# Seven block products for w_down in groups 2, 4 and 6 of a two-layer hybrid model in fp32

## The chip, the cores and the metric

The kernel runs on one core of a Trainium2 chip. The metric is the device time of one execution in microseconds (us); of several runs the median is given. The core has a matrix engine (PE, with its weight loads shown apart as PEld), a vector engine (DVE), a scalar engine (ACT), GpSimd (POOL) and a sync engine (SP). Each of them takes its own instructions in order. Transfers from memory are issued by SP or, where they add to what already lies in the target, by POOL.

## What is computed

The reference has two layers over x of 512 tokens by 1024 channels, all in fp32. In each layer a projection `w_in` feeds three mixers (mLSTM, differential attention, HGRN2), whose outputs go through `w_out` and are added to x. Then comes the part that the change touches:

```python
h2 = rmsnorm(x, norm2_g[l])
a = jnp.square(jax.nn.relu(jnp.einsum('btd,df->btf', h2, w_up[l])))
x = x + jnp.einsum('btf,fd->btd', a, w_down[l])
```

`w_up` is 1024 x 4096 and `w_down` 4096 x 1024. Every matrix product is made of three passes: each operand is split into a rounded part (hi, type fp32r) and the remainder (lo), and hi*hi, hi*lo and lo*hi are summed in PSUM.

## The kernel before

**Jobs and panels.** The work on weights is a list of jobs in a fixed order (the loop at the end of the kernel function). Each job multiplies by one panel of weights, 128 x 1024 fp32 (512 KB). The loop prepares panel n + 2 and then runs job n. Preparing means: SP loads the panel into a raw buffer, ACT rounds it to `whi` in two halves (line 243), DVE subtracts to get `wlo` in two halves (line 244). There are three buffers of `whi` and `wlo`, so that the ACT cast for job n + 2 can start when PE has ended job n - 1. A raw buffer is free again once DVE has made `wlo` from it. Preparation and the DVE additions out of PSUM have high priority in the order of instructions that the program writes for each engine.

**The feed-forward part.** The 4096 inner channels are cut into 8 groups of 512. Group 0 of `w_up` is an ordinary product (`up_first`). Groups 1 to 7 (`up_group`) use a seven-product block scheme in place of eight: 512 tokens are two halves, 512 channels two halves, 1024 inputs two halves; seven products of 256 x 512 x 256 with sums and differences of blocks. The sums of the activation blocks are made once per layer (`blocks`, names b11, t1, t2, ...). The sums of the weight blocks are made in the raw buffer by transfers that POOL issues with an add (`block_panel`, line 262): buffer `mA` holds w11 and then w11 + w21, buffer `kT` holds w21 + w22, then + w11, then + w12. Each of the two tags is a pair of halves, and group g uses half g % 2 of both, so that two groups in a row use different halves. The order of the seven products is p1, p5, p2, p7, p6, p4, p3. A product is 24 matmuls of 256 columns (lines 1130 to 1132) into PSUM tags `hx`, `ax` or `pv`; DVE adds it to others in `tmp`; and `relu2` (lines 1087 to 1091) does relu and square on ACT, a cast to `ah` on ACT and the remainder `al` on DVE. `S["ah"]` and `S["al"]` have two places, for even and odd groups.

**w_down.** `down_group` is an ordinary product by `nat_pair`: 4 panels, each a job of 24 matmuls of 512 columns (`nat_mm`, lines 295 to 297). Two jobs in a row sum in the same four PSUM tiles (tag `mm`, 4 buffers), which DVE adds to x at the end of the second (`add_rows`, line 1002).

**Order.** Jobs of down group g (letter d) and up group g + 1 (letter u) are interleaved by a string from `ORDER`: the first for g = 0, the second for g = 1 to 5, the third for g = 6; the four down jobs of group 7 stand alone.

Functions that have to be run between jobs (the block sums of `blocks`) stand in a list `steps`, of which one is run after each job.

Of the kernel before, what the change touches and what calls it, by code (L numbers as in the profile page):

```python
# [8 lines left out]
F32 = mybir.dt.float32  # L9
F32R = mybir.dt.float32r  # L10
U8 = mybir.dt.uint8
AF = mybir.ActivationFunctionType
# [3 lines left out]
P = 128  # L16
# [12 lines left out]
S4 = 1024  # L29
WP = 1056  # L30
WARM = 2
TOP = 1 << 24
ORDER = ("duduuduuduu", "uuduudududu", "uuuduuduudd")
RB = 3
COLS = dict(mq=0, mk=256, mv=512, mo=768, aq=1032, ak=1544, av=2056, hq=2568, hf=2824, hi=3080)

# [26 lines left out]
def hybrid_kernel(ctx, tc, x, norm1_g, w_in, conv_w, gate_b, mlstm_g, qn_g, kn_g, lam_v, subln_g,  # L63
                  lb_param, hgrn_g, w_out, norm2_g, w_up, w_down, cst, msk, out):
    nc = tc.nc
# [17 lines left out]
    xs = [pool.tile([P, D], F32, name=f"x{i}", tag=f"x{i}") for i in range(NT)]  # L83
# [19 lines left out]
    def pair(tag, dt=F32):  # L103

        return sb([P, 2 * S4], tag, dt)
# [137 lines left out]
            nc.scalar.copy(hi[:, ch], raw[:, ch])  # L243
            V.tensor_sub(lo[:, ch], raw[:, ch], hi[:, ch].bitcast(F32))  # L244

    def block_panel(raw, fresh, add):


        hi = sb([P, WP], "whi", F32R, bufs=3)
        lo = sb([P, WP], "wlo", F32R, bufs=3)  # L250

        def v3(t):
            return t[:, 0:S4].rearrange("p (k n) -> p k n", n=256)
# [495 lines left out]
    jobs = []  # L749
# [3 lines left out]
    steps = []  # L753

    def add_layer(l):
        S = {}
# [327 lines left out]

        NG = DFF // 512

        def relu2(src, r, q, ah, al):
            act(r, src, AF.Relu)
            act(q, r, AF.Square)
            nc.scalar.copy(ah, q)  # L1090
            V.tensor_sub(al, q, ah.bitcast(F32))

        def up_first():
            def ev(base):
                def f(pt, c, tok):
                    if base + c == 0 and tok.start == 0:
                        S["ah"] = [sb([P, 4, T], y, F32R) for y in HT[0:2]]
                        S["al"] = [sb([P, 4, T], y, F32R) for y in HT[2:4]]
                    relu2(pt, slab(0, T, off=T * c)[:, tok], slab(1, T, off=T * c)[:, tok],
                          S["ah"][0][:, base + c, tok], S["al"][0][:, base + c, tok])  # L1100
                return f
            for a in range(2):
                t_group(w_up, KT, a * 256, lambda: S["h2"], ev(2 * a), 2)

        def up_group(g):
# [8 lines left out]
            def raw(tag):  # L1114
                if "raw_" + tag not in S:
                    S["raw_" + tag] = pair(tag)
                return S["raw_" + tag][:, g % 2 * S4:(g % 2 + 1) * S4]

            def in_ring():
                return sb([P, WP], "wraw", bufs=2)  # L1120

            def product(wt, name, tag):
                pt = ps(tag)
                wh, wl = wt
                hh, hl = S["F"][name]
                for c in range(2):
                    col = slice(c * P, (c + 1) * P)
                    dst = pt[:, c * 256:(c + 1) * 256]
                    for k in range(4):
                        mm(dst, wh[:, k, col], hh[:, k], start=k == 0, stop=False)  # L1130
                        mm(dst, wh[:, k, col], hl[:, k], start=False, stop=False)  # L1131
                        mm(dst, wl[:, k, col], hh[:, k], start=False, stop=k == 3)  # L1132
                return pt

            def put(src, i, j):

                n = 2 * i + j
                tok = slice(j * 256, (j + 1) * 256)

                def two(v):  # L1140
                    return v.rearrange("p (c t) -> p c t", c=2)
                relu2(two(src), two(slab(0, 512, off=512 * (n % 2))), two(slab(1, 512, off=512 * (n % 2))),
                      S["ah"][g % 2][:, 2 * i:2 * i + 2, tok], S["al"][g % 2][:, 2 * i:2 * i + 2, tok])

# [12 lines left out]

            def p6(wt):
                V.tensor_sub(tmp[1], product(wt, "t2", "hx"), tmp[0])
                V.tensor_add(tmp[2], st["7"], tmp[1])  # L1160
                V.tensor_sub(tmp[0], tmp[2], st["5"])
                V.tensor_sub(tmp[3], st["5"], tmp[1])
                put(tmp[0], 1, 1)

            def p4(wt):
                if g == 4 and l + 1 < DEPTH:
                    load_gains(l + 1)
                    prms[l + 1] = load_params(l + 1)()
# [7 lines left out]
            return [((lambda: block_panel(raw("mA"), w[1, 1], [])), p1),  # L1176
                    ((lambda: block_panel(raw("kT"), w[2, 1], [w[2, 2]])), p5),
                    ((lambda: block_panel(in_ring(), w[1, 2], [])), p2),
                    ((lambda: block_panel(raw("mA"), None, [w[2, 1]])), p7),
                    ((lambda: block_panel(raw("kT"), None, [w[1, 1]])), p6),  # L1180
                    ((lambda: block_panel(in_ring(), w[2, 2], [])), p4),
                    ((lambda: block_panel(raw("kT"), None, [w[1, 2]])), p3)]
# [15 lines left out]
        up_first()  # L1198
        for g in range(NG):
            n = len(jobs)  # L1200
            down_group(g)
            if g + 1 < NG:
                down = jobs[n:]
                del jobs[n:]
                up = [(prep, None, None, go) for prep, go in up_group(g + 1)]
                for s in ORDER[min(g, 1) if g + 2 < NG else 2]:
                    jobs.append((up if s == "u" else down).pop(0))

    for l in range(DEPTH):
        add_layer(l)  # L1210
# [51 lines left out]
```

## Time and profile before

| | |
|---|---|
| median of 3 runs | 1284.72 us (1284.5 to 1285.47) |
| the profiled execution | 1284.39 us |
| its span, first to last instruction | 1282.6 us |
| granted TensorE clock | 1.00 of full speed |
| PE busy | 1271.0 us, 7492 matmuls |
| DVE busy | 914.8 us, 2064 instructions |
| ACT busy | 713.2 us, 1537 instructions |
| moved | 140.83 MB, of that 29.36 MB by POOL's queue |

The profiled execution is 1.8 us longer than its span and 0.33 us below the median. Busy time is the time in which an engine has at least one instruction under way. Matmuls overlap, so that the distance from one start to the next, not the length of one, tells what a matmul costs.

### The profile page before, as it was taken

The numbers are of one execution on the slowest core, as the hardware profiler recorded it, in microseconds if no ns is written. First come the engines' busy times: TensorE is split into PE (matmuls) and PEld (weight loads), VectorE is DVE, ScalarE is ACT, GpSimd is POOL, SyncE is SP. The second block draws the span as 40 slices with busy tenths as digits, with TensorE's granted clock in tenths as the row PEclk, the third lists the DMA queues.
The fourth block names the chain that finished last, engine by engine and source line by source line (L and its number), as shares of the span: only waits on it lengthen the run. The fifth ranks groups of instructions, "written<-read, shape, count | busy, mean of one in ns | idle before, by whom it ended". The sixth has DMA issues, their size and how long they took to land.

```text
span 1282.6 us, 20019 instructions
## 1 busy us (share of the span) xinstructions
PE 1271.0 (99%) x7492; PEld 1090.1 (85%) x7492; DVE 914.8 (71%) x2064; ACT 713.2 (56%) x1537; POOL 91.4 (7%) x92
## 2 busy tenths in 40 slices
PE   8999999999999999999999999999999999999998
PEld 6788777888999899889877887788898988898886
DVE  6786887978866666766567767878897657565763
ACT  6754875638655445445456557756485544444551
POOL 0000000000111111100000000000010111011100
PEclk9999999999999999999999999999999999999999
DMA  6222211226577576735323221112356765575552
GB/s 209 83 66 80 58 43 43 76 70 165 121 167 147 140 165 148 151 100 119 108 83 85 64 83 50 50 39 78 98 133 134 164 163 131 149 164 132 111 134 85
DMA packets 110228, 140.83 MB, mean 110 GB/s; under 512 B 5354, under 2 KB 79668, under 8 KB 110132
## 3 DMA queue, kind: packets, MB, share of 16 engines
q1 hardware_dynamic: 80228, 109.66, 28.0%
q0 software_dynamic: 29568, 29.36, 15.6%
q8 instruction: 59, 0.97, 0.3%
q10 hardware_dynamic: 336, 0.54, 0.1%
q14 instruction: 37, 0.30, 0.1%
HBM read 137.45 MB, written 2.10 MB: 109 GB/s over the span
## 4 chain that ended last, share of the span: by engine, by line
PE 88%; DVE 5%; ACT 4%; DMA 1%; issue 1%; SPq 0%; POOL 0%; ACTq 0%; DVEq 0%; POOLq 0%
PE pmm L295 15%; PE pmm L297 15%; PE pmm L296 15%; PE pmm L303 3%; PE pmm L304 3%; PE pax L1131 3%; PE pmm L302 3%; PE pax L1132 3%; PE pax L1130 3%; PE pax L685 2%; PE phx L1132 2%; PE ppv L1131 2%; PE phx L1131 2%; PE phx L1130 2%; PE ppv L1130 2%; PE ppv L1132 2%
## 5 line engine op out<-in xcount | busy, mean ns | idle before, releaser
L243 ACT CAST whi<-wraw 128x512 fp32r<-128x512 f32 x216 | 123.3, 617 | 181.6 <-PE pmm L297 140.5
L244 DVE TENSOR_TENSOR wlo<-wraw,whi 128x512 fp32r<-128x512 f32 x216 | 140.5, 688 | 75.7 <-ACT whi L243 75.7
L295 PE MATMUL pmm<-whi,h 128*128 128x512 f32 (+2 forms) x496 | 192.0, 387 | 0.2 <-ACT h L341 0.2
L296 PE MATMUL pmm<-wlo,h 128*128 128x512 f32 (+2 forms) x496 | 189.8, 383 | 0.0
L297 PE MATMUL pmm<-whi,h 128*128 128x512 f32 (+2 forms) x464 | 177.8, 383 | 0.0
L286 ACT ACTIVATE whi<-wraw,gcol 128x256 fp32r<-128x256 f32 (+2 forms) x192 | 99.5, 572 | 82.5 <-PE pmm L297 64.6
L287 DVE SCALAR_TENSOR_TENSOR wlo<-wraw,gcol,whi 128x256 fp32r<-128x256 f32 (+2 forms) x192 | 101.9, 570 | 47.8 <-ACT whi L286 46.1
L1002 DVE TENSOR_TENSOR x<-x,pmm 128x512 f32<-128x512 f32 x144 | 98.7, 686 | 45.5 <-PE pmm L297 43.4
L295 PEld LDWEIGHTS pmm<-whi,h 128*128 128x128 f32 x496 | 93.3, 188 | 16.9 <-ACT h L341 0.6
L296 PEld LDWEIGHTS pmm<-wlo,h 128*128 128x128 f32 x496 | 93.3, 188 | 16.7 <-issue 0.2
L297 PEld LDWEIGHTS pmm<-whi,h 128*128 128x128 f32 x464 | 87.2, 188 | 16.3
L295 PE MATMUL pmm<-whi,yb 128*128 128x512 f32 (+2 forms) x256 | 100.4, 392 | 0.0
L296 PE MATMUL pmm<-wlo,yb 128*128 128x512 f32 (+2 forms) x256 | 98.6, 385 | 0.0
L296 PE MATMUL pmm<-wlo,ya 128*128 128x512 f32 (+2 forms) x240 | 92.1, 384 | 0.0
L295 PE MATMUL pmm<-whi,ya 128*128 128x512 f32 (+2 forms) x240 | 92.1, 384 | 0.0
L297 PE MATMUL pmm<-whi,yd 128*128 128x512 f32 (+2 forms) x224 | 86.2, 385 | 0.0
L297 PE MATMUL pmm<-whi,yc 128*128 128x512 f32 (+2 forms) x224 | 85.6, 382 | 0.0
L262 POOL DMA_DIRECT2D kT<-in_w_up_dram x42 | 55.6, 1325 | 400.2 <-DVE wlo L244 241.7
L243 ACT CAST whi<-kT 128x512 fp32r<-128x512 f32 x84 | 48.0, 619 | 61.5 <-PE pmm L297 30.6
L1130 PE MATMUL phx<-mid,whi 128*128 128x256 f32 x224 | 63.0, 281 | 0.0
L1131 PE MATMUL phx<-mid,whi 128*128 128x256 f32 x224 | 62.9, 281 | 0.0
L1132 PE MATMUL phx<-mid,wlo 128*128 128x256 f32 x224 | 62.9, 281 | 0.0
(465 smaller groups left out, 3309.1 us busy)
## 6 DMA issues: line engine op xcount, KB each, us to landing
wraw<-in_w_down_dram SPq DMA_DIRECT2D x64, 512.0 KB
wraw<-in_w_in_dram SPq DMA_DIRECT2D x51, 512.0 KB
kT<-in_w_up_dram POOLq DMA_DIRECT2D x42, 512.0 KB, 6.2
wraw<-in_w_up_dram SPq DMA_DIRECT2D x36, 512.0 KB
wraw<-in_w_out_dram SPq DMA_DIRECT2D x16, 512.0 KB
mA<-in_w_up_dram SPq DMA_DIRECT2D x14, 512.0 KB
kT<-in_w_up_dram SPq DMA_DIRECT2D x14, 512.0 KB
mA<-in_w_up_dram POOLq DMA_DIRECT2D x14, 512.0 KB, 6.1
```

The lines of the kernel that those rows point to most:

```text
L243: nc.scalar.copy(hi[:, ch], raw[:, ch])
L244: V.tensor_sub(lo[:, ch], raw[:, ch], hi[:, ch].bitcast(F32))
L262: nc.gpsimd.dma_start(out=v3(raw), in_=rows(b), accum_op=ALU.add)
L286: act(hi[:, ch], raw[:, ch], AF.Copy, scale=g)
L287: V.scalar_tensor_tensor(lo[:, ch], raw[:, ch], g, hi[:, ch].bitcast(F32), op0=ALU.mult, op1=ALU.subtract)
L295: mm(pt[:, :n], sh(a), wh[:, b], start=first and j == 0, stop=False)
L296: mm(pt[:, :n], sh(a), wl[:, b], start=False, stop=False)
L297: mm(pt[:, :n], sl(a), wh[:, b], start=False, stop=last and j == nk - 1)
L1002: V.tensor_add(xs[i][:, cols], xs[i][:, cols], pt)
L1130: mm(dst, wh[:, k, col], hh[:, k], start=k == 0, stop=False)
L1131: mm(dst, wh[:, k, col], hl[:, k], start=False, stop=False)
L1132: mm(dst, wl[:, k, col], hh[:, k], start=False, stop=k == 3)
```

## The change

Down groups 2, 4 and 6 (`SEVEN`) are made by seven block products too (`down_seven`). The activations of the group are four blocks A11, A12, A21, A22 of 256 channels x 256 tokens, the panel of weights four blocks of 256 x 512. Each product is a job (letter s) of 12 matmuls of 512 columns, two PSUM tiles of tag `mm`. Three of the seven go straight to x, four go to accumulators `acc(0)` to `acc(3)` in SBUF, which sum over the three groups: in group 2 ACT copies them there, in groups 4 and 6 DVE adds. After group 6 two steps (`s0`, `s1`) combine the accumulators and add them to x.

`up_group` of an even group leaves the squared activations in `a4` in fp32; only two blocks are split at once, the block differences and sums are made by DVE and split (ACT cast and DVE remainder) at the end of p3 and of the first four down products. `S["ah"][0]` is cut into four places for them. In odd groups the square is made in place.

Raw buffers: the pair of halves is now `raw(0)`, `raw(1)` (first halves of `mA` and `kT`) for the up groups, which swap roles from group to group, and `raw(2)`, `raw(3)` (second halves) for the down groups. The order of the up products is p5, p1, p2, p7, p6, p4, p3. `ORDER` has a string for each g.

```diff
-ORDER = ("duduuduuduu", "uuduudududu", "uuuduuduudd")
+SEVEN = (2, 4, 6)
+ORDER = ("duduuduuduu", "uuduudududu", "usuusuusuus", "ususududusudud", "usuusuusuus", "ususududusudud", "usuusuusuus",
+         "sssdddd")
...
+        def split(ah, al, q):
+            nc.scalar.copy(ah, q)
+            V.tensor_sub(al, q, ah.bitcast(F32))
...
+        def raw(n):
+            t = ("mA", "kT")[n % 2]
+            if "raw_" + t not in S:
+                S["raw_" + t] = pair(t)
+            return S["raw_" + t][:, n // 2 * S4:(n // 2 + 1) * S4]
...
-                relu2(two(src), two(slab(0, 512, off=512 * (n % 2))), two(slab(1, 512, off=512 * (n % 2))),
-                      S["ah"][g % 2][:, 2 * i:2 * i + 2, tok], S["al"][g % 2][:, 2 * i:2 * i + 2, tok])
+                r = slab(0, 512, off=512 * (n % 2))
+                act(r, src, AF.Relu)
+                if g in SEVEN:
+                    act(a4()[:, n], r, AF.Square)
+                    if n in (0, 2):
+                        split(*place(n // 2), a4()[:, n])
+                else:
+                    act(r, r, AF.Square)
+                    split(S["ah"][1][:, 2 * i:2 * i + 2, tok], S["al"][1][:, 2 * i:2 * i + 2, tok], two(r))
...
                 put(tmp[3], 0, 1)
+                if g in SEVEN:
+                    a = a4()
+                    V.tensor_sub(a[:, 0], a[:, 0], a[:, 1])
+                    split(*place(2), a[:, 0])
+                    V.tensor_sub(a[:, 1], a[:, 1], a[:, 3])
+                    split(*place(3), a[:, 1])
...
+            one, two_ = (0, 1) if g % 2 else (1, 0)
+            return [((lambda: block_panel(raw(two_), w[2, 1], [w[2, 2]])), p5),
+                    ((lambda: block_panel(raw(one), w[1, 1], [])), p1),
                     ((lambda: block_panel(in_ring(), w[1, 2], [])), p2),
+                    ((lambda: block_panel(raw(one), None, [w[2, 1]])), p7),
+                    ((lambda: block_panel(raw(two_), None, [w[1, 1]])), p6),
                     ((lambda: block_panel(in_ring(), w[2, 2], [])), p4),
+                    ((lambda: block_panel(raw(two_), None, [w[1, 2]])), p3)]
+        def down_seven(g):
...
+            def product(wt, n, to, after=None):
+                hi, lo = (t.rearrange("p (k t) -> p k t", k=2) for t in place(n))
+                for c in range(2):
+                    pt = ps("mm")
+                    tok = slice(c * P, (c + 1) * P)
+                    nat_mm(pt, 512, lambda k: hi[:, k, tok], lambda k: lo[:, k, tok], *wt,
+                           [(0, 0), (1, 1)], True, True)
+                    with tc.high_priority():
+                        if isinstance(to, tuple):
+                            i, j = to
+                            d = xs[2 * j + c][:, i * 512:(i + 1) * 512]
+                            V.tensor_add(d, d, pt)
+                        elif g == SEVEN[0]:
+                            nc.scalar.copy(acc(to)[:, c], pt)
+                        else:
+                            V.tensor_add(acc(to)[:, c], acc(to)[:, c], pt)
+                if after:
+                    after()
...
+            return [(pan(one, w[1, 1], []), None, None, lambda t: product(t, 0, 0)),
+                    (pan(in_ring, w[1, 2], []), None, None, lambda t: product(t, 1, (0, 0), t2)),
+                    (pan(two, w[2, 1], [w[2, 2]]), None, None, lambda t: product(t, 2, 1, t4)),
+                    (pan(one, None, [w[2, 1]]), None, None, lambda t: product(t, 3, 3, b22)),
+                    (pan(two, None, [w[1, 1]]), None, None, lambda t: product(t, 0, 2)),
+                    (pan(in_ring, w[2, 2], []), None, None, lambda t: product(t, 1, (1, 0))),
+                    (pan(two, None, [w[1, 2]]), None, None, lambda t: product(t, 2, (0, 1), add_up))]
```

Here `t2` and `t4` are one DVE sum and one split each, `b22` one split; `one` is `raw(2)` and `two` is `raw(3)`. After group 6 `add_up` puts into `steps` two functions: `s0` with six DVE additions of 512 columns and one subtraction of 1024, `s1` with six of 512 and one of 1024.

## Rows read from the trace of the kernel before

**Rows 1.** The page: busy time of each engine and chain that ended last.
```profile
PE 1271.0 (99%) x7492; PEld 1090.1 (85%) x7492; DVE 914.8 (71%) x2064; ACT 713.2 (56%) x1537; POOL 91.4 (7%) x92
...
PE 88%; DVE 5%; ACT 4%; DMA 1%; issue 1%; SPq 0%; POOL 0%; ACTq 0%; DVEq 0%; POOLq 0%
```

**Rows 2.** Stretches of two groups each: busy us (instructions), clock, DMA share, GB/s.
```profile
core 0: us, PE busy (x) PEld busy (x) DVE busy (x) ACT busy (x) POOL busy (x), PEclk, DMA share, GB/s
...
494.00:578.00 84.00, 84.00 (x530) 75.73 (x529) 52.48 (x83) 40.13 (x71) 9.00 (x7) 1.00 0.62 138
...
1134.00:1218.00 84.00, 84.00 (x530) 75.34 (x529) 52.56 (x83) 40.22 (x71) 9.01 (x7) 1.00 0.58 133
```

**Rows 3.** Timeline of PE: first up job, then a down job, in layer 0 (start, length).
```profile
332.38 0.28 PE L1130 MATMUL phx<-mid,whi 128*128 128x256 f32 x1
...
335.22 0.40 PE L295 MATMUL pmm<-whi,h 128*128 128x512 f32 x1
...
340.76 0.28 PE L1130 MATMUL pax<-mid,whi 128*128 128x256 f32 x1
```

**Rows 4.** Timeline of ACT, then DVE, then POOL's queue: one panel's preparation.
```profile
408.27 1.14 ACT L243 CAST whi<-kT 128x512 fp32r<-128x512 f32 x2 [2.70 <-PE pmm L297]
...
408.93 1.29 DVE L244 TENSOR_TENSOR wlo<-kT,whi 128x512 fp32r<-128x512 f32 x2
...
410.52 1.28 POOL L262 DMA_DIRECT2D kT<-in_w_up_dram  x1 [3.02 <-DVE wlo L244]
```

**Rows 5.** Timeline of DVE: instructions that start one after the other without a wait.
```profile
480.21 0.69 DVE L1160 TENSOR_TENSOR big<-pax,big 128x512 f32<-128x512 f32 x1
480.93 0.69 DVE L1161 TENSOR_TENSOR big<-big,pax 128x512 f32<-128x512 f32 x1
481.54 0.69 DVE L1162 TENSOR_TENSOR big<-pax,big 128x512 f32<-128x512 f32 x1
```

**Rows 6.** Groups of DVE, 409 to 493 us: busy, mean ns, idle before and releaser.
```profile
L244 DVE TENSOR_TENSOR wlo<-wraw,whi 128x512 fp32r<-128x512 f32 x24 | 15.5, 686 | 8.7 <-ACT whi L243 8.7
L1002 DVE TENSOR_TENSOR x<-x,pmm 128x512 f32<-128x512 f32 x15 | 10.3, 686 | 4.3 <-PE pmm L297 4.2
...
L1091 DVE TENSOR_TENSOR h<-big,h 128x512 fp32r<-128x512 f32 x8 | 5.5, 691 | 6.9 <-ACT h L1090 6.9
L1152 DVE TENSOR_TENSOR big<-ppv,big 128x512 f32<-128x512 f32 x2 | 1.4, 692 | 1.8 <-PE ppv L1132 1.8
```

**Rows 7.** Timeline of ACT: cast of a panel, then relu, square, cast.
```profile
444.63 1.14 ACT L243 CAST whi<-mA 128x512 fp32r<-128x512 f32 x2 [1.57 <-PE ppv L1131]
445.68 0.63 ACT L1088 ACTIVATE big<-big 128x512 f32<-128x512 f32 x1
446.34 0.63 ACT L1089 ACTIVATE big<-big 128x512 f32<-128x512 f32 x1
```

**Rows 8.** Timeline of POOL, then of DVE, at the start of the feed-forward part, layer 0.
```profile
306.35 1.43 POOL L262 DMA_DIRECT2D kT<-in_w_up_dram  x1 [59.34 <-DVE wlo L287]
...
324.67 1.29 DVE L1043 TENSOR_TENSOR mid<-big,mid 128x512 fp32r<-128x512 f32 x2
325.87 1.22 DVE L1059 TENSOR_TENSOR big<-big 128x1024 f32<-128x1024 f32 x1
```

**Rows 9.** Timeline of POOL, and stretches around it (columns as in rows 2).
```profile
446.94 1.28 POOL L262 DMA_DIRECT2D mA<-in_w_up_dram  x1 [18.31 <-DVE wlo L244]
448.15 1.38 POOL L262 DMA_DIRECT2D kT<-in_w_up_dram  x1
...
449.00:455.00 6.00, 6.00 (x48) 5.79 (x47) 4.42 (x7) 3.10 (x6) 1.83 (x2) 1.00 1.16 171
...
459.00:461.00 2.00, 2.00 (x11) 1.60 (x10) 1.29 (x2) 0.83 (x2) 0.00 (x0) 1.00 0.87 298
```

**Rows 10.** Line 262 as a whole: from issue to landing.
```profile
DMA to landing us min/median/max: 6.0/6.2/12.7
```

**Rows 11.** Timeline of ACT: the cast that follows the transfer into `mA` of rows 9.
```profile
458.69 1.14 ACT L243 CAST whi<-mA 128x512 fp32r<-128x512 f32 x2 [1.15 <-PE pax L1131]
```

More of the change, by code (lines that the diff above doesn't have):

```diff
@@ L244, in halves, with block_panel @@
             V.tensor_sub(lo[:, ch], raw[:, ch], hi[:, ch].bitcast(F32))
-    def block_panel(raw, fresh, add):
+    def block_panel(raw, fresh, add, n=256):
         hi = sb([P, WP], "whi", F32R, bufs=3)
@@ L252, in v3 @@
         def v3(t):
-            return t[:, 0:S4].rearrange("p (k n) -> p k n", n=256)
+            return t[:, 0:S4].rearrange("p (k n) -> p k n", n=n)
         def rows(b):
@@ L1089, in relu2 @@
             act(q, r, AF.Square)
-            nc.scalar.copy(ah, q)
-            V.tensor_sub(al, q, ah.bitcast(F32))
+            split(ah, al, q)
         def up_first():
@@ L1103, in up_first, with in_ring, a4, place @@
                 t_group(w_up, KT, a * 256, lambda: S["h2"], ev(2 * a), 2)
+        def in_ring():
+            return sb([P, WP], "wraw", bufs=2)
+        def a4():
+            return slab(2, 2 * S4, (4, 512))
+        def place(n):
+            return S["ah"][0][:, n], S["al"][0][:, n]
+        def acc(n):
+            return slab((1, 4, 5, 6)[n], S4, (2, 512))
+        def raw(n):
[3 more added lines that the diff above has]
+            return S["raw_" + t][:, n // 2 * S4:(n // 2 + 1) * S4]
         def up_group(g):
@@ L1112, in up_group @@
             tmp = [slab(13 + n // 2, 512, off=512 * (n % 2)) for n in range(4)]
[L1114 to L1120, printed above, removed]
             def product(wt, name, tag):
@@ L1174, in p3 @@
                 put(tmp[3], 0, 1)
-            return [((lambda: block_panel(raw("mA"), w[1, 1], [])), p1),
-                    ((lambda: block_panel(raw("kT"), w[2, 1], [w[2, 2]])), p5),
+                if g in SEVEN:
[5 more added lines that the diff above has]
+            one, two_ = (0, 1) if g % 2 else (1, 0)
@@ L1178, in up_group @@
+            return [((lambda: block_panel(raw(two_), w[2, 1], [w[2, 2]])), p5),
+                    ((lambda: block_panel(raw(one), w[1, 1], [])), p1),
                     ((lambda: block_panel(in_ring(), w[1, 2], [])), p2),
-                    ((lambda: block_panel(raw("mA"), None, [w[2, 1]])), p7),
-                    ((lambda: block_panel(raw("kT"), None, [w[1, 1]])), p6),
+                    ((lambda: block_panel(raw(one), None, [w[2, 1]])), p7),
+                    ((lambda: block_panel(raw(two_), None, [w[1, 1]])), p6),
@@ L1181, in up_group, with t2, t4, b22 @@
                     ((lambda: block_panel(in_ring(), w[2, 2], [])), p4),
-                    ((lambda: block_panel(raw("kT"), None, [w[1, 2]])), p3)]
+                    ((lambda: block_panel(raw(two_), None, [w[1, 2]])), p3)]
+        def down_seven(g):
+            w = {(i, j): w_down[l, g * 512 + (j - 1) * 256:g * 512 + j * 256, (i - 1) * 512:i * 512]
+                 for i in (1, 2) for j in (1, 2)}
+            def product(wt, n, to, after=None):
[16 more added lines that the diff above has]
+                    after()
+            def t2():
+                a = a4()
+                V.tensor_add(a[:, 0], a[:, 0], a[:, 3])
+                split(*place(0), a[:, 0])
+            def t4():
+                a = a4()
+                V.tensor_sub(a[:, 0], a[:, 2], a[:, 0])
+                split(*place(1), a[:, 0])
+            def b22():
+                split(*place(2), a4()[:, 3])
+            def add_up():
+                def to_x(i, j, op, n):
+                    for c in range(2):
+                        d = xs[2 * j + c][:, i * 512:(i + 1) * 512]
+                        op(d, d, acc(n)[:, c])
+                def s0():
+                    to_x(0, 0, V.tensor_add, 0)
+                    V.tensor_sub(acc(2), acc(2), acc(0))
+                    to_x(0, 1, V.tensor_add, 1)
+                    to_x(0, 1, V.tensor_sub, 2)
+                def s1():
+                    V.tensor_add(acc(3), acc(3), acc(2))
+                    to_x(1, 0, V.tensor_add, 3)
+                    to_x(1, 1, V.tensor_add, 3)
+                    to_x(1, 1, V.tensor_sub, 1)
+                if g == SEVEN[-1]:
+                    steps.extend([s0, s1])
+            def pan(r, fresh, add):
+                return lambda: block_panel(r(), fresh, add, 512)
+            one, two = (lambda: raw(2)), (lambda: raw(3))
+            return [(pan(one, w[1, 1], []), None, None, lambda t: product(t, 0, 0)),
[5 more added lines that the diff above has]
+                    (pan(two, None, [w[1, 2]]), None, None, lambda t: product(t, 2, (0, 1), add_up))]
@@ L1198, in add_layer @@
         up_first()
+        todo = dict(u=[], d=[], s=[])
         for g in range(NG):
-            n = len(jobs)
-            down_group(g)
-            if g + 1 < NG:
[L1203 to L1207, printed above, removed]
+            if g in SEVEN:
+                todo["s"] += down_seven(g)
+            else:
+                n = len(jobs)
+                down_group(g)
+                todo["d"] += jobs[n:]
+                del jobs[n:]
+            if g + 1 < NG:
+                todo["u"] += [(prep, None, None, go) for prep, go in up_group(g + 1)]
+            jobs.extend(todo[s].pop(0) for s in ORDER[g])
     for l in range(DEPTH):
```

## The prediction

> **What bounds the kernel now.** First the page: PE is busy for 99% of the span and the chain that ended last lies on PE for 88% [rows 1]. Busy is no proof that PE is the limit, since matmuls overlap; so next the stretches of the feed-forward part. Over two groups (84 us) PE is busy all the time at full clock, while DVE works 52.5 us (83 instructions) and ACT 40 us [rows 2]. Then the timeline of PE: an up job starts at 332.38, the down job behind it at 335.22, the next at 340.76 [rows 3]. So an up job (24 matmuls of 256 columns) takes 2.84 us and a down job (24 of 512) 5.54 us, or 0.231 us a matmul. Seven up and four down jobs make 7 x 2.84 + 4 x 5.54 = 42.04 us, which is half of the 84 us of two groups: PE has no gap there. A matmul taken away from this part is worth 0.231 us, as long as nothing else comes to be late.
>
> How much room the others have is read from one panel's preparation: the cast starts when PE frees a buffer at 408.27, DVE ends at 410.22, POOL issues the next addition at 410.52 [rows 4]. That is 1.95 us, inside the two jobs (5.6 us) that run between the freeing and the panel's own job. 3.7 us are spare.
>
> **PE.** A down group had 4 x 24 = 96 matmuls of 512 columns; seven products have 7 x 12 = 84. 12 fewer, in 3 groups and 2 layers: 72 x 0.231 = 16.6 us saved. An s job takes 12 x 0.231 = 2.77 us.
>
> **DVE and ACT.** Per group of the new kind: seven panels in place of four give 6 more casts and 6 more remainders; 14 additions out of PSUM in place of 8 (group 2: 6, and 8 copies on ACT); in the up group 2 more DVE instructions, in t2, t4 and b22 five DVE and three ACT. That is 19 on DVE for groups 4 and 6, 11 for group 2, and 9 (group 2: 17) on ACT. At the end of the layer come 12 additions of 512 columns and 2 of 1024. DVE instructions that wait for nothing start 0.61 us apart, or 0.72 where one needs the result just before it [rows 5]; one of 1024 takes 1.22 [rows 8]. Per layer DVE gets 49 x 0.61 + 12 x 0.61 + 2 x 1.22 = 39.7 us more, about 79 in all.
>
> What hides them is PE's time, and it is not spread evenly. The strings for g = 2, 4, 6 (usuusuusuus) last 7 x 2.84 + 4 x 2.77 = 31.0 us and hold, for g = 4 and 6, on DVE: 22 remainders, 7 additions of the up products, 4 remainders in `put`, 8 additions of s products, 5 in t2, t4 and b22: 46 x 0.61 = 28.1 us, 91% of the stage, against 62% now. For g = 2 they are 40 (24.4 us). Counted job by job (4.6 instructions fit in a job of 2.8 us), the backlog is largest after u6, s and u4, at about 4 instructions or 2.4 us, below the 3.7 us spare. The strings for g = 3 and 5 last 50.4 us and hold 55 (33.6 us). I cost DVE at nothing; if its cover is gone, it costs what the second rival says.
>
> ACT: a cast of a panel takes 0.57 us of its pair's 1.14, a step of relu or square 0.66 from start to start [rows 7]. Fullest is g = 2 with 22 x 0.57 + 22 x 0.66 = 27 us of 31.0, then 23 us for g = 4 and 6: nothing. The last string (sssdddd) lasts 3 x 2.77 + 4 x 5.54 = 30.5 us; DVE has 28 x 0.61 + 9.8 = 26.9 us in it, and s0, which the additions of the second d job need, has the 5.54 us of the first d job for itself: nothing.
>
> A rule speaks against costing DVE at 0.61 an instruction. The Trainium skill, page VectorE: DVE Perf Modes, section The DRAIN you can't avoid, has the next instruction start only when the pipe is empty. By that rule 46 instructions would take 46 x 0.69 = 31.7 us, over the 31.0 of PE, and the sum would be some 3 us worse over four such stages. The trace does not agree: lengths of 0.69 start 0.61 apart [rows 5].
>
> **PSUM.** An s job takes two of four `mm` tiles and at least one job lies before the next s (but for the last string), so an addition may come 2.8 us late. No string puts an s between the two d jobs that share their tiles. Nothing.
>
> **The moved order of the up products.** p5 goes first and needs t1, made one step after b11. DVE ends t1 at 325.96, the first up job starts at 332.38 [rows 3, 8]. Its panel needs the addition issued at 306.35 [rows 8]; even with the longest landing of any, 12.7 us [rows 10], and 1.95 us of preparation it is ready at 321. Nothing.
>
> **Transfers.** SP's queue still loads four panels for each down group. POOL's gets four more additions per group, 24 in all (56 to 80), 12.6 MB more. Two additions together moved 171 GB/s between 449 and 455, 3.07 us for each panel of 524 KB; plain loads alone 298 GB/s, 1.76 us [rows 9]. A string usuusuusuus needs 6 additions and 7 loads: 18.4 + 12.3 = 30.7 us of 31.0. The next string has room (6 and 9: 34.3 of 50.4). So in three stages a layer the transfers are as full as DVE.
>
> Sharing the raw buffers takes lead away. u7's addition may start only when u1's panel has been read: u1's cast starts with the first job of the stage, DVE ends 1.95 us on, POOL issues 0.30 later [rows 4]. u7 runs five jobs (u s u u s, 14.06 us) after that start and its cast must start 1.95 us earlier. The landing may take 14.06 - 1.95 - 2.25 = 9.86 us. Now the same step has 458.69 - 446.94 = 11.75 us before the cast even wants to start [rows 9, 11], and 3.7 more. u6 to u3 is the same chain with the same five jobs. POOL's queue is in order: behind u7's addition wait those for u6 and s, and behind a late one all of them. Landings are 6.0 to 12.7 us, median 6.2 [rows 10]; two issued together were done at about 455, 7.0 us after the second issue [rows 9]. Bounds: nothing lost (landing 6.2 to 7.0), not less than nothing, as PE has no gap to give back; and 12.7 - 9.86 = 2.84 us for each of two chains in six stages, 34 us. Nearest are the two together; a third adds 3.07, so 10.1 us, 0.2 late, and with a load between 11.8, 2 us late. I take 0.5 us per stage: 3 us.
>
> **Sum.** 1284.4 (the profiled execution; 0.3 below the median) - 16.6 + 3 = 1270.8, against the median 1271.
>
> **Rivals.**
> First, the forecast: PE stays the bound, 1268 to 1276. For it: PE has no gap now, and every other engine fits below 100% in each stage.
>
> Second, DVE becomes the bound in the strings of g = 4 and 6. For it: 91%, in order, and it waits today for PE and ACT in short pieces that may stay: 6.9 us in two groups for a cast, 1.8 for PE at each of four kinds of addition [rows 6], together 7 us a group. Then a stage takes 28.1 + 7.0 = 35.1 us, 4.1 more than PE needs, and four such stages give back 16.4 us: 1284. Half of it gives 1276. Against it: these waits come where nothing else is ready, and there will be more that is. The rule on DRAIN named above, alone, would add 3 us and stay inside the forecast.
>
> Third, slower: the additions into the shared buffers land late. The place is u1 to u7 and u6 to u3 in usuusuusuus, the price what a landing takes over 9.86 us, twelve times. At 9.86 + 16.6 / 12 = 11.2 us it eats the whole gain; at the 12.7 of the longest row it gives 1284.4 - 16.6 + 34 = 1302. For it: 99% of transfer time in these stages. Against it: the median of 6.2 and the emptier stages between.
>
> Fourth, that the change does not do what it says: matmuls not fewer by 72. The counts above leave no room for it.
>
> **How the numbers follow.** Some 0.2% (2.6 us) is what a measurement of this kernel can tell from no change. The forecast has 0.66, all faster. The second has 0.17: 0.08 faster, 0.05 within, 0.04 slower. The third has 0.17: 0.03 faster, 0.03 within, 0.11 slower. Faster 0.77, within 0.08, slower 0.15. The time is the forecast's. The range starts at 1267.5, the full saving with nothing lost, and goes to 1282, which takes in the lighter half of the second and third; the rest, nearly 2 in 10, lies above.
>
> **What would show it.** In the profile after: 7420 matmuls, some 2190 instructions on DVE and 1607 on ACT, 80 additions by POOL. Right: PE busy without gaps in the strings usuusuusuus, each about 31 us, DVE above 85% there. Second rival: PE waiting for `wlo` while ACT's cast is long done and DVE never idle. Third: casts in line 243 waiting for a transfer into mA or kT, POOL's landings above 10 us, and PE gaps before u7 or u3. The prediction is wrong if these stages take over 33 us, or if gaps appear where I cost nothing (the first up job, the last string).

## The result and the profile after

The changed kernel takes 1270.42 us (median of four runs, 1269.62 to 1272.88) against 1284.85 us of the kernel before in runs beside it: a ratio of 0.9894, interval 0.9882 to 0.9906. The forecast was 1271.0 and faster. The profiled execution took 1270.51 us, 13.9 us less than the one of before; the span is 13.9 us shorter too.

The page, busy time by engine, transfers by POOL's queue and the chain that ended last:

```profile
span 1268.7 us, 20162 instructions
...
PE 1255.0 (99%) x7420; PEld 1076.1 (85%) x7420; DVE 987.2 (78%) x2190; ACT 748.4 (59%) x1607; POOL 120.5 (9%) x116
...
q0 software_dynamic: 36096, 41.95, 21.6%
...
PE 83%; DVE 6%; ACT 5%; DMA 3%; issue 1%; SPq 0%; POOL 0%; ACTq 0%; DVEq 0%; POOLq 0%
```

Against [rows 1], PE has 72 matmuls less and is still busy 99% of the span. POOL has 24 instructions more. PE's share of the chain fell from 88 to 83%, and DMA's rose from 1 to 3%: the first sign that a transfer is late somewhere.

One heavy string, usuusuusuus for g = 4 in layer 0, as a stretch (columns as in [rows 2]):

```profile
492.89:523.82 30.93, 30.93 (x217) 28.85 (x216) 27.32 (x45) 19.47 (x35) 6.37 (x5) 1.00 0.85 188
```

It lasts 30.93 us, PE has no gap in it, DVE works 88% of it. (The string for g = 6, from 574.96 to 605.94, has 28.62 us of DVE, 92%, and no gap of PE either.) This is what the sum rests on, and it holds.

**Where 2.7 us went.** 72 x 0.231 = 16.6 us less work on PE, 13.9 us less time: 2.7 us did not arrive. The same instruction of PE, a row sum after the feed-forward part of layer 0, in the kernel before and then in the changed one:

```profile
659.13 1.05 PE L790 MATMUL phx<-cst,nr 128*128 128x128 f32 x8
```
```profile
652.73 1.05 PE L792 MATMUL phx<-cst,nr 128*128 128x128 f32 x8
```

Layer 0 gained 6.40 of its 8.3 us, so 1.9 us are lost there and 0.8 in layer 1. (A second profile of the same kernel, c1 below, loses 1.5 and 1.3 us: how the loss is divided changes by half a microsecond from one execution to the next.) PE's timeline shows the places: the first down job in the string for g = 5, and the last string of each layer.

```profile
538.87 0.39 PE L297 MATMUL pmm<-whi,h 128*128 128x512 f32 x1
539.49 0.50 PE L298 MATMUL pmm<-wlo,h 128*128 128x512 f32 x1 [0.23 <-DVE wlo L246]
...
622.90 0.40 PE L297 MATMUL pmm<-whi,h 128*128 128x512 f32 x1
624.10 0.66 PE L340 MATMUL pax<-cst,x 128*128 128x128 f32 x4 [0.81 <-DVE x L1004]
...
1244.62 0.39 PE L298 MATMUL pmm<-wlo,yb 128*128 128x512 f32 x1
1245.32 0.50 PE L299 MATMUL pmm<-whi,yd 128*128 128x512 f32 x1 [0.30 <-DVE yd L1091]
```

Where a start follows 0.23 us after the last, PE works without a gap; here 0.62, 1.20 and 0.70 us lie between two starts (and 0.54 at 617.18, in the last string of layer 0). Behind the last of them stands this, in layer 1: POOL's addition for the panel of the seventh down product, then ACT, then DVE (start, length, instruction, idle before it):

```profile
1230.39 1.20 POOL L264 DMA_DIRECT2D kT<-in_w_down_dram  x1 [9.77 <-DVE wlo L246]
```
```profile
1236.29 1.14 ACT L245 CAST whi<-kT 128x512 fp32r<-128x512 f32 x2 [2.34 <-DMA kT<-in_w_down_dram]
```
```profile
1236.94 1.29 DVE L246 TENSOR_TENSOR wlo<-kT,whi 128x512 fp32r<-128x512 f32 x2 [1.46 <-ACT whi L245]
...
1243.38 0.68 DVE L1233 TENSOR_TENSOR x<-x,pmm 128x512 f32<-128x512 f32 x1
1243.98 1.29 DVE L1091 TENSOR_TENSOR yd<-big,yb 128x512 fp32r<-128x512 f32 x2
```

The fifth and the seventh down product share `raw(3)`. In "sss" at the head of the last string only one job lies between them. The addition for the seventh goes out when DVE has read the panel of the fifth, ACT waits 2.34 us for it and holds everything behind it in its order, DVE idles 1.46 us. Then DVE catches up with what has high priority (remainders, additions out of PSUM), and the split that the first d job needs, which has none, comes last, at 1243.98.

In layer 0 it is the same: ACT waits 2.22 us for this addition, DVE 1.20. The split of the first d job comes at 616.38. The sums of `s0` (line 1262 and the additions behind it; two had run before) start at 619.22, when that job is nearly over, and the addition into x for which PE's transposes at 624.10 wait comes behind them (timeline of DVE):

```profile
609.35 1.29 DVE L246 TENSOR_TENSOR wlo<-kT,whi 128x512 fp32r<-128x512 f32 x2 [1.20 <-ACT whi L245]
...
616.38 1.28 DVE L1091 TENSOR_TENSOR h<-big,h 128x512 fp32r<-128x512 f32 x2
...
619.22 1.22 DVE L1262 TENSOR_TENSOR big<-big 128x1024 f32<-128x1024 f32 x1
...
623.37 0.68 DVE L1004 TENSOR_TENSOR x<-x,pmm 128x512 f32<-128x512 f32 x1
```

Counted as in the prediction, the cast of the fifth panel starts with the last up job, and four jobs (u s s s, 11.15 us) run from there to the seventh product. Less 1.95 of preparation and 2.25 until the addition is out, its landing may take 6.95 us, where the chains in the heavy string have 9.86. It took 5.9 (1230.39 to 1236.29). So the limit was kept, and the seventh product itself is in time; what is spent is the lead of everything behind it on ACT and DVE.

At 538 it is a plain load that is late. POOL issued two additions at 525.61 and 526.81, SP the loads of two down panels at 529.58; ACT and the transfers then show:

```profile
536.89 1.14 ACT L245 CAST whi<-wraw 128x512 fp32r<-128x512 f32 x2 [3.83 <-DMA wraw<-in_w_down_dram]
```
```profile
528.00:531.00 3.00, 3.00 (x21) 2.70 (x21) 2.90 (x6) 1.14 (x2) 0.14 (x1) 1.00 1.03 175
531.00:534.00 3.00, 3.00 (x21) 2.69 (x20) 0.59 (x1) 0.59 (x1) 0.00 (x0) 1.00 1.20 223
```

DMA engines are full (shares 1.03 and 1.20), and ACT's cast waits 3.83 us for a load that has no addition. All in all, ACT now waits for transfers in this way:

```profile
ACT whi L245 <- DMA wraw<-in_w_down_dram: 24.9, 7, 4.5
...
ACT whi L245 <- DMA kT<-in_w_up_dram: 14.1, 8, 2.3
...
ACT whi L245 <- DMA mA<-in_w_up_dram: 9.1, 6, 2.1
```

(us in total, times, longest.) In the heavy strings the lead of the panels swallows them; in the two places above it does not. In the median, landings are hardly longer than before [rows 10]. But apart from the two at the head of each feed-forward part, 8 of 76 take more than 9 us (10.8 at most), against 1 of 52 before; four of the 8 are in heavy strings, where PE has no gap:

```profile
DMA to landing us min/median/max: 5.8/6.5/12.2
```

### The profile page after: what moved, and what is told of

Same layout as the page of the kernel before. It is cut to its first block, busy times and chain, and to the rows that moved or that the text cites. A ratio compares the mean times of both kernels' runs of the same rounds, so it can differ in the third digit from the quotient of the medians.

```text
span 1268.7 us, 20162 instructions
## 1 busy us (share of the span) xinstructions
PE 1255.0 (99%) x7420; PEld 1076.1 (85%) x7420; DVE 987.2 (78%) x2190; ACT 748.4 (59%) x1607; POOL 120.5 (9%) x116
## 4 chain that ended last, share of the span: by engine, by line
PE 83%; DVE 6%; ACT 5%; DMA 3%; issue 1%; SPq 0%; POOL 0%; ACTq 0%; DVEq 0%; POOLq 0%
PE pmm L299 14%; PE pmm L297 14%; PE pmm L298 14%; PE pmm L305 3%; PE pmm L306 3%; PE pmm L304 3%; PE pax L1148 3%; PE pax L1147 3%; PE pax L1149 3%; PE pax L687 2%; PE phx L1148 2%; PE phx L1149 2%; PE phx L1147 2%; PE ppv L1147 2%; PE ppv L1148 2%; PE ppv L1149 2%
## 5 line engine op out<-in xcount | busy, mean ns | idle before, releaser
L297 PE MATMUL pmm<-whi,h 128*128 128x512 f32 (+2 forms) x484 | 187.3, 387 | 0.1
L245 ACT CAST whi<-wraw 128x512 fp32r<-128x512 f32 x192 | 109.4, 618 | 123.9 <-PE pmm L299 64.1
L299 PE MATMUL pmm<-whi,h 128*128 128x512 f32 (+2 forms) x452 | 173.3, 383 | 0.1
L246 DVE TENSOR_TENSOR wlo<-wraw,whi 128x512 fp32r<-128x512 f32 x192 | 125.7, 687 | 45.5 <-ACT whi L245 45.4
L245 ACT CAST whi<-kT 128x512 fp32r<-128x512 f32 x108 | 61.6, 618 | 52.5 <-DMA kT<-in_w_up_dram 14.1
L298 PE MATMUL pmm<-wlo,ya 128*128 128x512 f32 (+2 forms) x228 | 87.3, 383 | 0.0
L246 DVE TENSOR_TENSOR wlo<-kT,whi 128x512 fp32r<-128x512 f32 x108 | 69.6, 685 | 19.0 <-ACT whi L245 18.4
L1004 DVE TENSOR_TENSOR x<-x,pmm 128x512 f32<-128x512 f32 x96 | 65.5, 683 | 22.4 <-PE pmm L299 21.4
L245 ACT CAST whi<-mA 128x512 fp32r<-128x512 f32 x92 | 52.4, 617 | 48.9 <-PE pmm L299 21.5
L264 POOL DMA_DIRECT2D kT<-in_w_up_dram x30 | 38.9, 1298 | 409.9 <-DVE wlo L246 248.2
L246 DVE TENSOR_TENSOR wlo<-mA,whi 128x512 fp32r<-128x512 f32 x92 | 59.3, 685 | 13.6 <-ACT whi L245 13.6
```

Source lines behind the costliest of these rows:

```text
L1004: V.tensor_add(xs[i][:, cols], xs[i][:, cols], pt)
```

## The experiments

Theory at the outset: PE is still the bound, and the 2.7 us are lost at the end of each layer to `s0` and `s1`. The rival: late additions into the shared raw buffers. All ratios are against runs of the kernel before on the same chip (1284.3 to 1284.6 us).

**e1, without the sums at the end.**

```diff
-                    steps.extend([s0, s1])
+                    pass
```

> Leaves out s0 and s1 (the accumulators are never added to x). Theory: of the 16.6 us that PE saves, some 2.7 do not arrive, and most of that is the last string of layer 0 and 1, where 9.8 us of additions on DVE stand between the last products and the additions into x: PE gaps of 0.4 us at 617, 1.0 us at 623 and 0.5 us at 1244. Without them 1268.5 us (1.9 less than the changed kernel's 1270.4), no PE gap in front of the transposes of the next layer. Rival (the loss is late transfers): 1270.4, and the same gap of 0.8 us in front of the first d of g = 5.

Measured: 1270.80 us, ratio 0.9893 (0.9879 to 0.9906), the same as the whole change. The gap at 622 us goes, the one at 1244 is longer than above:

```profile
1244.95 0.50 PE L299 MATMUL pmm<-whi,yd 128*128 128x512 f32 x1 [1.22 <-DVE yd L1091]
```

The second profile of the changed kernel, with the sums, has nearly the same there, so that this gap tells nothing about them:

```profile
1245.31 0.50 PE L299 MATMUL pmm<-whi,yd 128*128 128x512 f32 x1 [0.96 <-DVE yd L1091]
```

So the theory that the sums cost 1.9 us falls. They have a part in the gap at 622, 1 us at most, but only since DVE is late there for another reason: in e2, which keeps them, it goes too.

**e2, down panels without POOL's additions.**

```diff
-                    (pan(two, w[2, 1], [w[2, 2]]), None, None, lambda t: product(t, 2, 1, t4)),
+                    (pan(two, w[2, 1], []), None, None, lambda t: product(t, 2, 1, t4)),
```

and so for the other three panels.

> Leaves out the 24 additions of POOL in the down panels (blocks of weights instead of their sums). Theory: the transfers cost only the 0.8 us in front of the first d job of g = 5 in layer 0, where a plain load shares with two additions and takes 7.2 us: 1269.6, ACT's waits for transfers shrink from 53 us to under 25. Rival (late additions cost in small pieces in all six stages, as the prediction's 3 us had it): 1267.8 or less. Second rival (DVE is what costs): 1270.4.

Measured: 1268.20 us, ratio 0.9875 (0.9862 to 0.9889). By the medians that is 16.3 us less than the kernel before, so that nearly all of the 16.6 arrive. (The span of the profiled execution, 1265.8, is even 2.9 us below that of the changed kernel, but it was the fastest of the four.) The interval overlaps with that of the changed kernel, though of the four times only one, 1269.72, is above the lowest of that kernel's eight, 1269.62. The gaps of both last strings are gone. DVE does the same there in the same order, as its timeline in layer 0 shows, but no longer stands in front of the seventh product's remainder, and the split comes at 614.27 in place of 616.38:

```profile
607.35 1.29 DVE L246 TENSOR_TENSOR wlo<-kT,whi 128x512 fp32r<-128x512 f32 x2
...
614.27 1.29 DVE L1091 TENSOR_TENSOR h<-big,h 128x512 fp32r<-128x512 f32 x2
```

The gap at 538 remains:

```profile
538.12 0.40 PE L297 MATMUL pmm<-whi,h 128*128 128x512 f32 x1
538.72 0.50 PE L298 MATMUL pmm<-wlo,h 128*128 128x512 f32 x1 [0.20 <-DVE wlo L246]
```

The rival stands in the main: the additions into the down buffers cost most of what is missing. It is not spread over all six stages, as that rival had it, but lies in the last strings. The run takes away the chain in the buffer and 12.6 MB of transfers at once and does not separate the two. ACT's waits for panels fell only from 53 to 45 us, not to under 25, so that most of them cost PE nothing. The gap at 538, some 0.5 us, is not due to these additions. Its plain load comes late in both kernels; why was not followed further.

**e5, the raw buffers and the order of the up products alone.** The kernel before, with only these two edits:

```diff
-                return S["raw_" + tag][:, g % 2 * S4:(g % 2 + 1) * S4]
+                return S["raw_" + tag][:, 0:S4]
...
-            return [((lambda: block_panel(raw("mA"), w[1, 1], [])), p1),
-                    ((lambda: block_panel(raw("kT"), w[2, 1], [w[2, 2]])), p5),
+            return [((lambda: block_panel(raw(two_), w[2, 1], [w[2, 2]])), p5),
+                    ((lambda: block_panel(raw(one), w[1, 1], [])), p1),
```

> The kernel before with the new order of the up products and the shared raw halves, without the seven products for w_down. Theory: with the long d jobs between, every addition has its 14 us and more, and PE has no gap: 1284.7, within 1 us. Rival (the lead that is lost costs also here): 1287 or more.

Measured: 1285.56 us (11 runs), ratio 1.0008 (0.9999 to 1.0017). Sharing the buffers and moving p5 cost 0.2% at most, with the old strings, whose down jobs of 5.5 us give each addition more time. The upper end, 2.2 us, is not far from the 2.7 that are missing; that they cost little in the changed kernel too rests on e2, which has both and loses next to nothing.

**e6, groups 4 and 6 only.** Group 2 of each layer stays an ordinary product.

```diff
-SEVEN = (2, 4, 6)
+SEVEN = (4, 6)
```

with the strings of the kernel before for g = 2 and 3.

> Seven products for groups 4 and 6 only; group 2 as before (and the old string for g = 2 and 3). Theory: what is saved is 48 matmuls of 0.231 us, 11.1 us, less some 1.5 us of the loss: 1275 to 1276, so that group 2 is worth some 5 us in two layers like the others. Rival (the string of group 2, where ACT takes eight additions from DVE, gives more than the others because DVE limits those): 1277 or more.

Measured: 1276.81 us, ratio 0.9946 (0.9934 to 0.9959), between the theory (up to 1276) and its rival (1277 or more). **The changed kernel again**, beside it:

> The changed kernel as it is, beside the others of this call: 1270.4 us by every theory.

It took 1271.09 us, ratio 0.9898 (0.9884 to 0.9911). The third group in a layer is worth 5.7 us, against 24 x 0.231 = 5.5 by count. (In e6 group 4 is the first and has ACT's copies, so it is one group with DVE's additions that is taken out.) The other two bring 7.5 us of their 11.1: the loss is not smaller with fewer groups, as far as figures tell that are known to some 2 us each. The profiled execution of e6, the slowest of five, has the gaps in the last strings too, up to 1.88 us between two starts.

**e3, two more DVE instructions in each s job.** A maximum of a constant tile with itself ahead of each addition out of PSUM, meant to fill DVE.

```diff
+                        for _ in range(1):
+                            V.tensor_max(nmask, nmask, nmask)
```

> Adds two DVE instructions of 512 columns to every s job (a maximum of a constant with itself), 14 per group. Theory: DVE is 91% full in the strings of g = 4 and 6; with 46 + 8 = 54 instructions of 0.61 us it needs 32.9 us against 31.0 and becomes the bound there: 1.9 us x 4 = 7.8 us more, 1278. Rival (the buffers of panels let the emptier strings take the surplus): less than 1 us more, 1270.4 to 1271.4.

Measured: 1318.08 us, ratio 1.0262 (1.0248 to 1.0276). It tells nothing about the heavy strings: the time was lost in the mixers, in layer 0 between 200 and 260 us, where all 42 maxima of the layer ran, and the heavy string for g = 4 still lasted 31 us. The maxima depend on nothing in the s jobs, and with high priority the program had put them early.

**e7 and e8, the same on an accumulator.** Groups 4 and 6 only; fourteen instructions of 512 columns for each in e7, twice as many in e8.

```diff
+                        for r in range(1 if g != SEVEN[0] else 0):
+                            e = acc(3 - r)[:, c]
+                            V.tensor_max(e, e, e)
```

In e8 the range is 2.

> Two more DVE instructions of 512 columns in every s job of groups 4 and 6 (a maximum of an accumulator with itself, which changes nothing), so that only the feed-forward part can move. Theory: 46 + 8 = 54 instructions of 0.61 us are 32.9 us in strings of 31.0: DVE becomes the bound, 1.9 us in each of four, 1278. Rival (the panels' lead and the emptier strings take the surplus): 1270.4 to 1271.5.

> The same with four more DVE instructions in every s job of groups 4 and 6: 46 + 16 = 62 instructions are 37.8 us against 31.0. Theory: 6.8 us in each of four strings, 1297. Rival (the emptier strings take it): less than 4 us more, under 1275.

Measured: 1313.27 us (ratio 1.0217, 1.0201 to 1.0233) and 1316.76 us (1.0257, 1.0243 to 1.0271): 42 us for the first dose, 3.5 more for the second. Not a price for work. The timelines of e7's DVE and POOL tell why:

```profile
442.18 4.48 DVE L1232 TENSOR_TENSOR big<-big 128x512 f32<-128x512 f32 x7
446.57 0.69 DVE L246 TENSOR_TENSOR wlo<-kT,whi 128x512 fp32r<-128x512 f32 x1
```
```profile
442.13 1.21 POOL L264 DMA_DIRECT2D kT<-in_w_down_dram  x1 [1.62 <-DVE wlo L246]
449.60 1.32 POOL L264 DMA_DIRECT2D kT<-in_w_up_dram  x1 [6.26 <-ACT whi L245]
```

`acc(3)` is complete early, so eight maxima ran a string ahead of their jobs, seven of them in one block in front of the remainder of a panel in `kT`. In the changed kernel the same addition went out 4.3 us earlier:

```profile
445.26 1.32 POOL L264 DMA_DIRECT2D kT<-in_w_up_dram  x1 [2.32 <-DVE wlo L246]
```

In e7 it is late, ACT waits for it, PE waits for ACT and DVE, and then PE itself is slow (timelines of ACT and PE, and stretches):

```profile
459.87 1.14 ACT L245 CAST whi<-kT 128x512 fp32r<-128x512 f32 x2 [3.93 <-DMA kT<-in_w_up_dram]
```
```profile
461.87 0.49 PE L298 MATMUL pmm<-wlo,h 128*128 128x512 f32 x1 [4.28 <-DVE wlo L246]
...
463.38 0.63 PE L297 MATMUL pmm<-whi,h 128*128 128x512 f32 x1
463.81 0.63 PE L298 MATMUL pmm<-wlo,h 128*128 128x512 f32 x1
```
```profile
457.00:461.80 4.80, 0.59 (x3) 0.15 (x1) 1.28 (x3) 1.93 (x4) 0.00 (x0) 1.00 0.29 75
461.80:466.30 4.50, 4.43 (x12) 3.50 (x13) 3.10 (x6) 2.13 (x4) 0.00 (x0) 0.62 0.72 226
466.30:470.00 3.70, 3.70 (x25) 3.35 (x24) 1.00 (x2) 1.14 (x2) 1.28 (x1) 1.00 0.44 153
```

The d job of 24 matmuls lasted 11.67 us in place of 5.54: 4.45 us of gap and 1.7 us at the lower clock. The addition also took longer to land than its like in the changed kernel (issue to landing, first e7, then the changed kernel):

```profile
DMA to landing us min/median/max: 10.2/10.2/10.2
```
```profile
DMA to landing us min/median/max: 6.3/6.3/6.3
```

So one addition into a shared buffer, issued 4.3 us late and 3.9 us longer under way, cost 6.1 us.

**e10, the same DVE work that cannot move.** Fourteen maxima again, but each on the tile that the eviction has just written.

```diff
+                        if g != SEVEN[0]:
+                            e = d if isinstance(to, tuple) else acc(to)[:, c]
+                            V.tensor_max(e, e, e)
```

> The changed kernel with the same count of added DVE work as in the run with two more per s job (fourteen maxima of 512 columns for each of groups 4 and 6, 56 in all), but each one works on the very tile that the eviction before it has just written, so it cannot run earlier than its own job. The output is unchanged. In the earlier run the maxima worked on an accumulator that was already complete, and its DVE timeline shows eight of them in one block from 442.18 to 447.86, a whole string before their jobs, in front of the remainder of a panel in kT; POOL's next addition into kT was issued at 449.60 in place of 445.26 us. Theory A (what cost 42 us there was that block, which made additions into the shared buffers late): here the maxima stay in their jobs. DVE has 28.1 + 8 x 0.61 = 33.0 us of work in each of the four heavy strings of groups 4 and 6 against 30.93 us of PE, so 0 to 2 us each: 1271 to 1279 us. Theory B (the added DVE work itself costs, through waits that stay with every DVE instruction): as there, over 1300 us, with gaps of about 4 us.

Measured: 1282.49 us (ten runs; the profiled one 1280.35), ratio 0.9985 (0.9974 to 0.9995). Theory B falls: 31 us of e7's 42 came from where the maxima stood. A is a little over its bound (11.4 us more than the changed kernel, not 0 to 8). The two heavy strings of layer 0, as stretches, and PE after the first:

```profile
493.00:524.00 31.00, 31.00 (x218) 28.91 (x218) 29.70 (x49) 17.51 (x33) 6.37 (x5) 1.00 0.87 190
577.30:608.24 30.94, 30.94 (x217) 28.72 (x216) 29.87 (x50) 17.88 (x32) 5.00 (x4) 1.00 0.63 122
```
```profile
541.71 0.50 PE L298 MATMUL pmm<-wlo,h 128*128 128x512 f32 x1 [2.10 <-DVE wlo L246]
```

DVE is at 96 and 97%, and no gap of PE lies inside either string. What DVE cannot do there it does behind it, and PE then waits 2.1 us in the string for g = 5 and some 3.5 us in all in the last one. Of the 4.9 us that were added to the first string (8 x 0.61), 2.4 fit in (29.70 against 27.32).

49 instructions in 29.70 us are 0.606 us each. By the rule of the Trainium skill named in the prediction (page VectorE: DVE Perf Modes, section The DRAIN you can't avoid) 49 of 0.69 us would take 33.8 us, more than the stretch. The prediction left out that the same section lets an instruction that is not held, that is, need not wait until all before it have finished, start earlier; the trace agrees with that exception and not with the rule taken alone.

**e4, jobs in a row.** Only the order of the jobs changes.

```diff
-"usuusuusuus", "ususududusudud",
+"uuuuuuussss", "sssuuuuuuudddd",
```

> The same kernel with the s jobs in a row: uuuuuuussss for g = 2, 4, 6 and sssuuuuuuudddd for g = 3, 5. Theory: the interleaving matters by the lead of the additions: from u6's panel to u3's only four up jobs (11.36 us) are left, so that a landing may take 7.2 us where it takes 6.5 to 7.3 in the middle; 0.5 to 1.5 us lost in each of six stages, 1273 to 1279, with casts waiting for transfers into mA and kT. Rival (DVE alone counts, and its sum per stage is unchanged): 1270.4.

Measured: 1385.09 us, ratio 1.0788 (1.0773 to 1.0802), span 1389.2 in the profiled run at a mean clock of 0.965. All expectations were far off: interleaving is worth 114 us, eight times what the change gains. The first of many gaps, in ACT, PE and stretches:

```profile
428.33 1.14 ACT L245 CAST whi<-kT 128x512 fp32r<-128x512 f32 x2 [4.12 <-DMA kT<-in_w_up_dram]
```
```profile
432.82 0.55 PE L1147 MATMUL pax<-yd,whi 128*128 128x256 f32 x1 [4.74 <-DVE big L1184]
433.18 0.42 PE L1148 MATMUL pax<-yd,whi 128*128 128x256 f32 x1
433.39 0.41 PE L1149 MATMUL pax<-yd,wlo 128*128 128x256 f32 x1
```
```profile
428.00:433.00 5.00, 0.26 (x2) 0.21 (x2) 3.99 (x7) 3.22 (x6) 0.63 (x1) 0.87 1.08 213
433.00:438.00 5.00, 5.00 (x24) 5.00 (x25) 3.40 (x6) 1.88 (x3) 0.56 (x1) 0.50 0.97 198
```

In a row, p1 to p7 and p6 to p3 have four up jobs from cast to product, 4 x 2.84 = 11.36 us, so 7.2 us for the landing in place of 9.86; two additions together took 7.0 before the change [rows 9], and one behind another of the same chain has to wait for it. This is a count; no run tests these two chains by themselves. PE stands for 4.7 us and then starts matmuls of 256 columns 0.21 us apart, where 0.118 is usual, at half clock.

**e9, e4 without POOL's additions in the down panels** (the edits of e4 and e2 together).

> The s jobs in a row as in the run that took 1385 us, and leaves out the 24 additions of POOL in the down panels (blocks of weights instead of their sums). Theory: most of the 115 us lost there are additions into one buffer whose readers are two s jobs apart (w21 + w22, then + w11, then + w12), each some 5 us of PE gap and a slower clock behind it; without them less than half of the loss is left (the up jobs' own additions): 1290 to 1325. Rival (it is DVE's work in a crowd of s jobs): 1370 or more.

Measured: 1338.70 us, ratio 1.0415 (1.0401 to 1.0429): between the two expectations. The 24 additions carry 46 of the 114 us; the other 68, which the additions for the up jobs and the rest of the order share, were not separated.

**v1, the last three s jobs interleaved.** The whole change, but with the string for g = 6 holding all seven s jobs and the last one only the d jobs, so that the fifth and the seventh have more jobs between them.

```diff
-"usuusuusuus",
-         "sssdddd")
+"ususususususus",
+         "dddd")
```

> The changed kernel with the last three s jobs of group 6 moved between up jobs (ususususususus for g = 6, then dddd). Theory: in the last string sss, ACT stands 2.3 us at a cast for the addition between s4's and s6's panel, which share one buffer and are two jobs apart; DVE falls behind with the remainders that the first d job needs. With four jobs between, the gaps of PE at 617 and 1244 go: 1268 to 1269. Rival: 8 additions and 8 loads need 38.6 of this string's 39.3 us, and the transfers lose more there than the last string did: 1271 or more.

Measured: 1269.49 us (1268.73 to 1270.83), ratio 0.9887 (0.9873 to 0.9900), 1.6 us below the changed kernel run again beside it, with intervals that overlap. ACT waits for no addition into a down panel any more, and in layer 0 the gap of about 1 us at 622 is gone. In layer 1 one of 1.1 us stays at the first d job, no shorter than in the second profile of the changed kernel: the job now waits for ACT's cast of the activations, and ACT has stood 2.94 us for a plain load before. So the distance explains ACT's wait for the addition, but not all that PE loses; that full transfers take the rest remains open. If anything this order is the better of the two.

## Why the prediction was right

**PE's saving, right.** 72 matmuls x 0.231 us = 16.6 us: the counts came as forecast (7420, 2190 and 1607 instructions, 80 additions), e2 shows 16.3 us by the medians once the additions are away, and e6 gives 5.7 us for two groups of the six against 5.5.

**DVE at nothing, right, with less room than the sum of a string suggests.** The heavy strings last 30.93 us with PE full and DVE at 88% (forecast 91). The second rival, that waits in short pieces stay (7 us a group), falls: e10 puts DVE to 96% and more, and PE still has no gap inside the heavy strings of layer 0. The margin was near the truth: 31.0 - 28.1 = 2.9 us free, and 2.4 more went in.

**Transfers and shared buffers: the size right by luck, the place wrong.** I took 3 us, 0.5 for each of six heavy strings; 2.7 us did not arrive, and e2 shows that POOL's additions into the down buffers take most of it, but in other strings. But I named the chains u1 to u7 and u6 to u3 in usuusuusuus, and there nothing is lost: ACT waits up to 2.3 us for `kT` and `mA` and the lead of the panels absorbs it. The step that failed is the one on the last string, which I costed at nothing from the sum of DVE's work (26.9 of 30.5 us). What it missed is distance, not work: the fifth and the seventh down product have four jobs and 6.95 us, not five and 9.86. The addition kept even that, with 5.9 us, but ACT stood 2.34 us for it and DVE 1.46 behind ACT, in a string that DVE's work nearly fills. `s0`, which I gave the first d job for itself, ran for the most part at the end of that job and behind it. I worked out the landing limit for two chains and did not go through all the pairs that share a buffer. The text had the right alarm ("gaps where I cost nothing: the first up job, the last string"); the last string is where it rang.

**The sums `s0` and `s1` at nothing, right as far as the times tell.** e1 without them takes the same time. In layer 0 they make the late DVE later still, and the gap at 622 goes without them, but it also goes without the additions.

**The moved order of the up products at nothing, right.** e5 bounds it, with the sharing, at +0.2% (2.2 us) at most with the old strings.

**The third rival's mechanism is real, only small here.** I priced it from the longest landing (12.7 us). In the median the landings hardly changed (6.5 us), but more of them are long, up to 10.8 us in the middle of the feed-forward part: a sign that I named for this rival, and one that cost PE nothing in the heavy strings. In e4 the addition of the first gap landed after 6.3 us, so that it was its late issue, with the buffer's reader too near, that made it late; in e7 late issue and long landing came together. There the price is what rival three said and more, since the clock falls behind the gaps shown.

## What to carry to other kernels

For each buffer that a chain of transfers reuses, count the jobs from one reader's cast to the next reader, for every pair and in every string, and set their time against preparation plus landing; a sum of work over the stage does not show it. When a stage is filled to 90% by an engine, look for the loss in what comes behind it, where the backlog is paid. And when work is added to measure a price, tie it to the data of its place, or the program moves it and something else is measured.

## What was not expected of the hardware

Two gaps of PE cost more than their length. In e7, 4.3 us of waiting were followed by matmuls of 512 columns 0.43 us apart in place of 0.23 and a mean granted clock of 0.62 over the next 4.5 us (1.2 GHz for most of it, before it rose back to 2.4). In e4 a gap of 4.7 us was followed by 5 us at a clock of 0.50. The gaps of the changed kernel, of at most 1.2 us between two starts, and e10's of 2.1 us, had a clock of 1.00 or close to it (mean 1.00 and 0.998 over the run). Over e4's span a mean clock of 0.965 is at most 1389.2 x 0.035 = 49 us of the 120 by which this execution is longer than the profiled one of the changed kernel, an estimate.
